# Attention opening in another order, and second-projection weights in dead tiles of keys and queries

## The chip, the core and the metric

The kernel runs on one core of a Trainium2 chip. The metric is the device time of one launch in microseconds (us). The core has five engines with a queue of instructions each: TensorE (PE: matrix products and transposes into PSUM), VectorE (DVE), ScalarE (ACT), GpSimd (POOL) and SyncE (SP), which here only issues DMAs. An engine works its queue in order; an instruction whose inputs are not there holds all that stands behind it. DMAs of one queue are carried out by 16 shared DMA engines.

## The reference

Two layers work on 512 latent tokens and 256 context tokens of 1024 channels. In each layer a modulated RMS norm feeds one projection whose columns go to three groups: Fourier mixing (256 channels), neighbourhood attention (6 heads of 64) and gated linear attention (GLA, 4 heads). The three outputs are joined, go through one output projection with a gated residual, and a modulated norm with a SwiGLU FFN (hidden size 2816) follows. Condensed:

```python
def na_latent(q, k, v, kc, vc, rpb):          # window of the grid + all context keys
    s_loc = einsum('bhrqd,bhrakd->bhrqak', qg, kb) * scale + bias     # masked outside the window
    s_ctx = einsum('bhrqd,bnhd->bhrqn', qg, kc) * scale
    p = jax.nn.softmax(jnp.concatenate([s_loc, s_ctx], -1), axis=-1)
    ...
def fourier_mix(u, w):                        # Re(2-D DFT over positions and group channels)
    return jnp.fft.fftn(z, axes=(1, 3), norm="ortho").real.reshape(B, L, FN_W) @ w
...
x = x + gate * (concat([fourier, attention, gla]) @ w_out)
x = x + gate2 * swiglu(ada_modulate(x))       # the FFN
```

In layer 0 both streams are updated; in layer 1, the last, only the latent one is needed.

## The kernel before

Everything is in fp32. Each product is made of three passes over operands that are split into a high part (ScalarE copies it out as `fp32r`) and a low part (VectorE or GpSimd subtracts the high part): `mm3` (line 183) issues the three, `split` (197) makes the parts. A weight tile is loaded as `raw` (`wraw`, 428) and split into `whl` (`wsplit`, 433), so a weight costs a DMA, an ACT copy and a DVE or POOL subtraction before TensorE can use it.

The output projection is cut in two. The first part, with weights `woa` (five blocks of 128 rows: GLA and Fourier channels), is the generator `wo`; its products are spread over the attention by `fill`, which takes them as filler between the attention's own products. The second part, weights `wob` (three blocks: the attention's channels), is the generator `wb` and runs when the attention is over. Both come from `wout` (969). It makes 8 output tiles `m` for each stream `n`; a product ends with an addition to the residual (`stt`, names `u<-m,u,u` and the like). `raws` are the loaded tiles, two at a time; `part` splits one. In layer 1 `wb` is `whole`: all eight tiles are split beforehand into `whlw`, through two `raw` buffers. In layer 0 it isn't: a tile is split as the one before it is used.

The opening of the attention: line 1111 onward. `next(wo)` issues the first two `woa` loads and the first split; `load_heads` brings keys and queries (`kn`, `qn`, six tiles of 128x512 each) from memory; `load_bias` the position bias; `fourier` (`fn`) makes the Fourier group's features (`ab`, then `pe`, `raw` and `u`), and `stacks_of_heads` (`first`) transposes keys and queries of the first pair of heads and stacks them (`st`). `load_heads("v", vn)` and `load_streams` follow, which load the residual streams `xc` (`u<-in_cxt`) and `xl` (`u<-in_xt`, in layer 1 `u<-xs`). The attention itself goes through 3 pairs of heads in 5 (layer 1: 4) blocks: scores (`a<-st,st`), bias and maximum (`s`, `mx`), exponential (`p`), reciprocal (`rcl`), transposes (`b<-u,p`), copies to `pT`, values (`y<-pT,vn`). While one pair runs, the next pair's keys and queries are prepared (`kt`, `qt`). `kn` and `qn` are dead when the third pair's are prepared.

After the attention the FFN begins: `norm_add` sums squares (`nsq`, `nacc`; for the latent stream of layer 0 on GpSimd), `norm_sums` and `norm_spread` make the norm's factor (`nms`, `nrs`, `ndg`), `nt` and `u<-nt` are the normalised inputs, and `W_first` loads and splits the FFN's first four weight tiles on GpSimd.

The order of the work: on TensorE it is written by hand in the attention and the second projection (`manual_schedule`); on the other engines a scheduler with a model of the times sets it when the program is built. `issue_after` holds instructions back until another one. Pools lay tiles over one another, and a tile that is laid where another was waits until that one is read for the last time.

## Time and profile before

| what | value |
|---|---|
| median of 3 runs | 1663.78 us (1663.53 to 1668.41) |
| profiled execution | 1662.66 us, span 1660.6 us |
| TensorE busy | 1613.8 us (97%) |
| VectorE, ScalarE, GpSimd busy | 920.6 (55%), 583.9 (35%), 232.2 (14%) |
| DMA | 199.66 MB, mean 120 GB/s |
| mean granted TensorE clock | 0.995 |

TensorE is busy nearly all the time, so the time is its work and its pauses. In the slices of the page its share is full in all but the first; the pauses show only in finer windows and in the timeline, where a row's bracket gives the idle time ahead of it and what ended it.

### The profile page before, as it was taken

The page shows a single profiled execution, that of the slowest core. Times are in us where ns is not written, and L with a number is a line of the kernel's source. Part 1 is how long each engine was busy: PE and PEld are TensorE (multiplying, and loading weights), DVE is VectorE, ACT ScalarE, POOL GpSimd, SP SyncE. Part 2 cuts the span into 40 slices and gives each one's busy share as a digit, 9 for nine tenths or more (in the row PEclk, how much of TensorE's full clock was granted, in tenths as well). Part 3 has the DMA queues.
Part 4 walks back from the last instruction along what each step waited for, and adds up shares of the span by engine and source line. Part 5 has one row for each costly group of instructions (what it writes and reads, how often), then busy time and mean ns, then how long its engine had stood idle before and what let it go on. Part 6 is the DMA issues. An engine that isn't in the chain of part 4 may idle for free.

```text
span 1660.6 us, 25071 instructions
## 1 busy us (share of the span) xinstructions
PE 1613.8 (97%) x9938; PEld 1402.3 (84%) x9938; DVE 920.6 (55%) x1665; ACT 583.9 (35%) x1048; POOL 232.2 (14%) x275
## 2 busy tenths in 40 slices
PE   6999999999999999999999999999999999999999
PEld 5878889787888888888888889899787988888887
DVE  5699974776774664355333434464577743434432
ACT  5365223544542411211122324842445522222220
POOL 0143431003240400000000011333102000000000
PEclk9999999999999999999999999999999999999999
DMA  9445544653152454144221411222663233233321
GB/s 329 159 151 164 164 155 124 192 134 112 52 175 76 153 188 143 62 148 146 65 75 45 127 53 40 70 97 94 194 182 119 84 113 99 91 93 98 102 89 51
DMA packets 79904, 199.66 MB, mean 120 GB/s; under 512 B 10344, under 2 KB 21164, under 8 KB 78764
## 3 DMA queue, kind: packets, MB, share of 16 engines
q1 hardware_dynamic: 79788, 198.07, 37.9%
q8 instruction: 78, 1.28, 0.3%
q14 instruction: 38, 0.31, 0.1%
HBM read 174.84 MB, written 14.29 MB: 114 GB/s over the span
## 4 chain that ended last, share of the span: by engine, by line
PE 81%; DVE 7%; DMA 6%; ACT 2%; issue 2%; SPq 1%; POOL 0%; DVEq 0%; ACTq 0%; POOLq 0%
PE a L181 26%; PE m L181 23%; PE b L181 19%; PE y L181 11%; DVE adac L192 2%; DMA adaw<-in_adaw 2%; DVE u L192 1%; DVE whl L189 1%; PE b L1244 1%; DMA raw<-in_wg 1%; DMA raw<-in_wob 1%; DMA raw<-in_w 1%; ACT whl L195 1%; DMA qn<-scr_q 1%; DVE u L189 1%
## 5 line engine op out<-in xcount | busy, mean ns | idle before, releaser
L195 ACT ACTIVATE whl<-raw 128x1024 fp32r<-128x1024 f32 (+7 forms) x222 | 205.0, 928 | 392.2 <-PE a L181 132.3
L189 DVE TENSOR_TENSOR whl<-raw,whl 128x1024 fp32r<-128x1024 f32 (+7 forms) x201 | 225.2, 1122 | 91.7 <-ACT whl L195 91.5
L181 PE MATMUL m<-u,whl 128*128 128x512 f32 (+1 forms) x1278 | 264.1, 359 | 1.9 <-DVE whl L189 1.9
L181 PE MATMUL a<-u,whl 128*128 128x512 f32 (+1 forms) x1299 | 246.6, 346 | 2.4 <-ACT u L195 1.5
L181 PEld LDWEIGHTS m<-u,whl 128*128 128x128 f32 x1278 | 211.9, 191 | 35.3 <-DVE whl L189 2.2
L181 PEld LDWEIGHTS a<-u,whl 128*128 128x128 f32 x1299 | 208.6, 189 | 32.6 <-ACT u L195 1.7
L181 PE MATMUL b<-u,whl 128*128 128x512 f32 (+1 forms) x915 | 181.8, 349 | 1.8 <-ACT whl L195 0.9
L192 DVE SCALAR_TENSOR_TENSOR adac<-adaw,u,adac 128x512 f32<-128x512 f32 x196 | 159.0, 828 | 42.1 <-DMA adaw<-in_adaw 41.0
L181 PEld LDWEIGHTS b<-u,whl 128*128 128x128 f32 x915 | 150.1, 189 | 25.2 <-ACT whl L195 1.1
L181 PE MATMUL b<-whl,u 128*128 128x384 f32 (+1 forms) x696 | 144.9, 345 | 1.3 <-DVE u L192 0.9
L181 PE MATMUL m<-whl,u 128*128 128x384 f32 (+2 forms) x672 | 138.0, 344 | 2.8 <-ACT u L195 2.5
L181 PEld LDWEIGHTS b<-whl,u 128*128 128x128 f32 x696 | 122.2, 189 | 8.7 <-issue 4.7
L181 PEld LDWEIGHTS m<-whl,u 128*128 128x128 f32 x672 | 116.5, 189 | 15.3 <-issue 9.8
L181 PE MATMUL a<-g,whl 128*128 128x512 f32 (+1 forms) x594 | 126.9, 370 | 0.7 <-DVE g L189 0.7
L181 PEld LDWEIGHTS a<-g,whl 128*128 128x128 f32 x594 | 103.9, 189 | 19.8 <-DVE g L189 1.2
L181 PE MATMUL y<-u,whl 128*128 128x512 f32 (+1 forms) x420 | 83.6, 353 | 1.0 <-DVE u L189 1.0
L192 DVE SCALAR_TENSOR_TENSOR ft<-ft,a 128x512 f32<-128x512 f32 (+1 forms) x53 | 30.5, 576 | 95.0 <-ACT ft L195 63.0
L181 PEld LDWEIGHTS y<-u,whl 128*128 128x128 f32 x420 | 69.2, 192 | 12.7 <-DVE u L189 1.4
L181 PE MATMUL m<-g,whl 128*128 128x512 f32 (+1 forms) x396 | 77.8, 350 | 0.0
L181 PEld LDWEIGHTS m<-g,whl 128*128 128x128 f32 x396 | 64.8, 189 | 9.7
L181 PE MATMUL b<-g,whl 128*128 128x256 f32 (+1 forms) x396 | 72.4, 336 | 0.0
L189 POOL TENSOR_TENSOR nacc<-nacc,nsq 128x512 f32<-128x512 f32 (+1 forms) x14 | 15.0, 1074 | 400.2 <-ACT nsq L195 400.2
(220 smaller groups left out, 1983.6 us busy)
## 6 DMA issues: line engine op xcount, KB each, us to landing
raw<-in_w SPq DMA_DIRECT2D x104, 512.0 KB, 3.9
adaw<-in_adaw SPq DMA_DIRECT2D x48, 512.0 KB, 3.8
adaw<-in_adaw SPq DMA_DIRECT2D x64, 256.0 KB, 3.0
raw<-in_wg SPq DMA_DIRECT2D x40, 384.0 KB, 3.4
raw<-in_w SPq DMA_DIRECT2D x32, 448.0 KB, 3.4
adaw<-in_ada SPq DMA_DIRECT2D x8, 1024.0 KB, 10.5
st<-kt SPq DMA_DIRECT2D x32, 192.0 KB, 4.1
raw<-in_woa SPq DMA_DIRECT2D x16, 320.0 KB, 8.8
```

The lines of the kernel that those rows point to most:

```text
L181: last_mm[0] = T.matmul(o, lhsT=l, rhs=r, start=start, stop=stop, skip_group_check=True).ins
L189: e.tensor_tensor(out=o, in0=a, in1=b, op=op)
L192: V.scalar_tensor_tensor(out=o, in0=a, scalar=s, in1=b, op0=op0, op1=op1)
L195: S.activation(out=o, in_=i, func=f, **kw)
L1244: T.transpose(ps[:, 128 * j:128 * j + 128], p[:, 128 * j:128 * j + 128], ident)
```

## The change

The change has five parts. (1) `next(wo)` goes from before the loads of keys and queries to behind those of the bias. (2) With `hold`, the addition of the first product waits for the second product. (3) In layer 1 the queries' transposes are no longer held back behind the Fourier group's last steps. (4) The tags `s`, `p` and `pT` are allocated first in their pool, so `pT` lies elsewhere. (5) `places`: the loads and splits of `wob` use the dead tiles of `kn` and `qn`; in layer 0 five of the eight are split during the attention, tiles 5 and 6 in the buffers of `wo`, and from tile 5 on (before: 6) the products go stream by stream; in layer 1 all eight are loaded without waiting for a buffer.

```diff
+        def place(n):
+            return mk(nap, [128, 512], F32, [f"kn{j}" for j in range(6)][n] if n < 6 else f"qn{n - 6}")
-        def wout(src, nk, streams, kinds, whole=False, split_at=KD, begin=0):
+        def wout(src, nk, streams, kinds, whole=False, split_at=KD, begin=0, places=None, hold=False):
...
+            def raw(m):
+                if places is None:
+                    return wraw(wop, src[m], 128 * nk, 2, cap)
+                r = place(m if whole else m % 2)[:, :128 * nk]
+                nc.sync.dma_start(out=r, in_=src[m])
+                return r
+            def part(r):
+                m = len(w)
+                if places is None or whole or m in (5, 6):
+                    return wsplit(wop, r, (nk, 128), nb, cap, tag)
+                hh, ll = [place(2 + 2 * (m % 5 if m < 5 else 0) + i)[:, :128 * nk].bitcast(F32R) for i in range(2)]
+                split(r, hh, ll)
...
             if whole:
-                w = [part(raw(m)) for m in range(KD)]
+                with tc.issue_after(last_stack[0]):
+                    raws = [raw(m) for m in range(KD)]
+                for r in raws:
+                    w.append(part(r))
+            elif places:
+                raws = [raw(m) for m in range(2)]
+                for m in range(5):
+                    w.append(part(raws[m]))
+                    raws.append(raw(m + 2))
...
-                stt(xs(m), ps, gm(s, m), xs(m), ALU.mult, ALU.add)
+                held.append(lambda: stt(xs(m), ps, gm(s, m), xs(m), ALU.mult, ALU.add))
+                if hold and (m, n) == (0, 0):
+                    return
+                for add in held:
+                    add()
+                held.clear()
...
-        next(wo)
         load_heads("k", kn)
         load_heads("q", qn)
...
             load_bias(nap, h)
+        next(wo)
...
+        for tag, shape, bufs in (("s", [128, 512], 2), ("p", [128, 512], 4), ("pT", [128, 4, 128], 3)):
+            mk(np_, shape, F32, tag, bufs)
...
-        wb = wout(d["wob"][l], 3, streams, "mbmya", not ctx_q, 6 if ctx_q else 0, 0 if ctx_q else 4)
+        wb = wout(d["wob"][l], 3, streams, "mbmya", not ctx_q, 5 if ctx_q else 0, 0 if ctx_q else 4, True)
...
-                if loaded and not ahead:
+                if n == 2 * nb and not ahead:
                     ahead.append(next(wb))
```

Three places show what this moves. The first is SyncE's queue in the opening of layer 0, from the last row of the Fourier tables to the values (`raw<-in_woa` are the first projection's weights). Before:

```order
L1085 DMA pe_3260<-in_nyq 1x258
L430 DMA raw_3108<-in_woa 128x640
L430 DMA raw_3110<-in_woa 128x640
L893 DMA kn_625_3087<-scr_k_35_118 128x1x512
L893 DMA kn_626_3088<-scr_k_35_118 128x1x512
```

and the same stretch after, up to where the two loads now stand:

```order
L1115 DMA pe_3260<-in_nyq 1x258
L893 DMA kn_625_3087<-scr_k_35_118 128x1x512
...
L891 DMA qn_636_3098<-scr_q_37_120 128x512
L1151 DMA bias_3161<-in_rpb 128x512
L1151 DMA bias_3164<-in_rpb 128x512
L430 DMA raw_3167<-in_woa 128x640
L430 DMA raw_3169<-in_woa 128x640
L893 DMA vn_619_3081<-scr_v_36_119 128x1x384
```

The two loads have moved behind all loads of keys, queries and bias. Their splits on ScalarE have moved too, in the same opening; after the change they stand among the feature copies (`u<-m` context features, `ab` latent features, `st` key stacks):

```order
L195 ACTIVATE u_3058<-m_3217 128x256
L195 ACTIVATE whl_3171<-raw_3167 128x640
L195 ACTIVATE u_3059<-m_3218 128x256
L195 ACTIVATE ab_669_3277<-y_3264 128x512
L195 ACTIVATE ab_671_3293<-a_3280 128x512
L195 ACTIVATE whl_3478<-raw_3169 128x640
L195 ACTIVATE st_616_3078<-a_3311 128x256
```

Before, both splits stood eleven and eight rows ahead of `u_3058<-m_3217`, so nothing between these rows waited for a weight.

The second place is GpSimd at the handover from layer 0's second projection to the FFN. `whl` are the first FFN weights' low parts, `nacc` the sums of squares, `nrs` the reciprocal roots. Before:

```order
L189 TENSOR_TENSOR whl_4955<-raw_4953,whl_4955 128x1024
L189 TENSOR_TENSOR whl_4960<-raw_4958,whl_4960 128x1024
L189 TENSOR_TENSOR whl_4965<-raw_4963,whl_4965 128x1024
L189 TENSOR_TENSOR whl_4970<-raw_4968,whl_4970 128x1024
L189 TENSOR_TENSOR nacc_4649<-nacc_4649,nsq_4712 128x512
L189 TENSOR_TENSOR nacc_4649<-nacc_4649,nsq_4745 128x512
```

and after:

```order
L189 TENSOR_TENSOR nacc_4679<-nacc_4679,nsq_4905 128x512
L189 TENSOR_TENSOR nacc_4679<-nacc_4679,nsq_4926 128x512
L189 TENSOR_TENSOR whl_4964<-raw_4962,whl_4964 128x1024
L189 TENSOR_TENSOR whl_4969<-raw_4967,whl_4969 128x1024
L189 TENSOR_TENSOR nrs_5076<-nms_5074,u_63 128x4
L189 TENSOR_TENSOR whl_4974<-raw_4972,whl_4974 128x1024
L189 TENSOR_TENSOR whl_4979<-raw_4977,whl_4979 128x1024
```

The four splits have gone from ahead of the first of seven additions to behind the last.

The third is ScalarE in the third pair of layer 1 (`whlw` are splits of the second projection's weights, `p` exponentials, `pT` copies of transposed probabilities). Before:

```order
L195 ACTIVATE p_12261,sml_12262<-s_12257,nm_12259 128x512
L195 ACTIVATE whlw_12475<-raw_12473 128x384
L195 ACTIVATE pT_12331<-b_12326 128x512
L195 ACTIVATE p_12309,sml_12310<-s_12305,nm_12307 128x512
L195 ACTIVATE whlw_12480<-raw_12478 128x384
L195 ACTIVATE p_12320,sml_12321<-s_12316,nm_12318 128x512
```

and after:

```order
L195 ACTIVATE p_12273,sml_12274<-s_12269,nm_12271 128x512
L195 ACTIVATE whlw_12368<-kn_2207_12352 128x384
L195 ACTIVATE whlw_12371<-kn_2208_12354 128x384
L195 ACTIVATE whlw_12374<-kn_2209_12356 128x384
L195 ACTIVATE whlw_12377<-kn_2210_12358 128x384
L195 ACTIVATE whlw_12380<-kn_2211_12360 128x384
L195 ACTIVATE pT_12343<-b_12338 128x512
L195 ACTIVATE p_12321,sml_12322<-s_12317,nm_12319 128x512
L195 ACTIVATE whlw_12383<-kn_2212_12362 128x384
```

Five splits stand where one stood in front of the copy to `pT`. On VectorE the first product's addition, in the opening of layer 0, has not moved: `u<-m,u,u` 128x256 stands behind `kt<-b` and ahead of the first `rcl` in both.

## Rows read from the trace of the kernel before

**Rows 1.** The page, part 1: the span, and the tensor engine's busy time and instructions.
```profile
span 1660.6 us, 25071 instructions
PE 1613.8 (97%) x9938; PEld 1402.3 (84%) x9938; DVE 920.6 (55%) x1665; ACT 583.9 (35%) x1048; POOL 232.2 (14%) x275
```

**Rows 2.** Windows: stretch, length, PE busy (instructions), granted clock, DMA share, GB/s.
```profile
280.00:300.00 20.00, 19.61 (x148) 1.00 0.75 215
400.00:410.00 10.00, 8.14 (x39) 0.84 0.62 199
1240.00:1250.00 10.00, 8.44 (x69) 1.00 0.82 195
```

**Rows 3.** Timeline, TensorE, layer 0's handover: start, length, what, [idle before, releaser].
```profile
397.51 1.33 PE L181 MATMUL y<-u,whl 128*128 128x256 f32 x9 [0.95 <-DVE u L189]
...
406.02 1.46 PE L181 MATMUL m<-u,whl 128*128 128x256 f32 x8 [1.86 <-DVE whl L189]
...
411.79 2.23 PE L181 MATMUL m<-u,whl 128*128 128x512 f32 x9
...
414.93 2.23 PE L181 MATMUL m<-u,whl 128*128 128x512 f32 x9
...
426.31 2.33 PE L181 MATMUL y<-u,whl 128*128 128x512 f32 x9
...
442.38 3.16 PE L181 MATMUL b<-u,whl 128*128 128x256 f32 x25
445.38 0.86 PE L181 MATMUL m<-u,whl 128*128 128x512 f32 x3
```

**Rows 4.** Timeline, TensorE, layer 1's opening and third pair.
```profile
1200.63 1.19 PE L181 MATMUL a<-st,st 128*128 128x512 f32 x4 [2.83 <-DVE st L192]
...
1249.30 1.20 PE L181 MATMUL a<-st,st 128*128 128x512 f32 x4 [1.56 <-DMA raw<-in_wob]
...
1254.07 1.09 PE L181 MATMUL y<-pT,vn 128*64 128x128 f32 x16
```

**Rows 5.** Timeline, TensorE, layer 0's opening.
```profile
293.38 0.51 PE L181 MATMUL m<-whl,ab 128*128 128x258 f32 x2
...
309.13 0.66 PE L1244 MATMUL b<-u,p 128*128 128x128 f32 x4 [2.90 <-DVE p L1223]
```

**Rows 6.** Timeline, VectorE, layer 0's opening.
```profile
307.52 0.48 DVE L192 SCALAR_TENSOR_TENSOR u<-m,u,u 128x256 f32<-128x256 f32 x1 [0.88 <-DMA u<-in_cxt]
```

**Rows 7.** The chain of waits in the same opening: start, length, what.
```profile
280.68 11.56 DMA qn<-scr_q
...
300.00 7.50 DMA u<-in_cxt
```

**Rows 8.** Timeline, SyncE's DMA issues, same opening.
```profile
271.98 0.25 SPq L1085 DMA_DIRECT2D pe<-in_nyq  x1
275.33 1.01 SPq L430 DMA_DIRECT2D raw<-in_woa  x2
```

**Rows 9.** Timeline, ScalarE, same opening.
```profile
292.71 0.62 ACT L195 ACTIVATE ab<-y 128x512 fp32r<-128x512 f32 x1
```

**Rows 10.** Timeline, VectorE, layer 0's handover.
```profile
403.55 2.42 DVE L189 TENSOR_TENSOR whl<-raw,whl 128x384 fp32r<-128x384 f32 x1 [1.04 <-ACT whl L195]
...
417.99 0.55 DVE L189 TENSOR_TENSOR whl<-raw,whl 128x384 fp32r<-128x384 f32 x1
...
430.58 1.66 DVE L192 SCALAR_TENSOR_TENSOR u<-nt,u,u 128x256 fp32r<-128x256 f32 x2 [0.38 <-ACT u L195]
```

**Rows 11.** Timeline, GpSimd, layer 0's handover.
```profile
403.18 7.69 POOL L189 TENSOR_TENSOR whl<-raw,whl 128x1024 fp32r<-128x1024 f32 x3 [2.74 <-DMA raw<-in_w]
...
430.29 1.27 POOL L189 TENSOR_TENSOR nacc<-nacc,nsq 128x512 f32<-128x512 f32 x1 [1.27 <-ACT nsq L195]
```

**Rows 12.** Timeline, ScalarE, layer 1's third pair.
```profile
1250.04 0.53 ACT L195 ACTIVATE whlw<-raw 128x384 fp32r<-128x384 f32 x1 [3.80 <-DMA raw<-in_wob]
1251.03 0.60 ACT L195 ACTIVATE pT<-b 128x512 f32<-128x512 f32 x1 [0.47 <-PE b L1244]
```

More of the change, by code (lines that the diff above doesn't have):

```diff
@@ L965, in hybrid_kernel @@
         gm = lambda s, k: modT[l][:, s, 16 + k:17 + k]
-        loaded = []
-        def wout(src, nk, streams, kinds, whole=False, split_at=KD, begin=0):
+        def place(n):
+            return mk(nap, [128, 512], F32, [f"kn{j}" for j in range(6)][n] if n < 6 else f"qn{n - 6}")
+        def wout(src, nk, streams, kinds, whole=False, split_at=KD, begin=0, places=None, hold=False):
             nb, cap = (KD, 128 * nk) if whole else (2, 640)
             tag = "whl" + "w" * whole
-            raw = lambda m: wraw(wop, src[m], 128 * nk, 2, cap)
-            part = lambda r: wsplit(wop, r, (nk, 128), nb, cap, tag)
-            if whole:
-                w = [part(raw(m)) for m in range(KD)]
+            def raw(m):
[10 more added lines that the diff above has]
+                split(r, hh, ll)
+                return [a.rearrange("p (a b) -> p a b", a=nk) for a in (hh, ll)]
+            w = []
+            if whole:
+                with tc.issue_after(last_stack[0]):
[7 more added lines that the diff above has]
+                    raws.append(raw(m + 2))
             else:
                 raws = [raw(m) for m in range(2)]
-                w = [part(raws[0])]
+                w.append(part(raws[0]))
             early = {}
@@ L1003, in product @@
                         yield None, ps.shape[-1]
-                stt(xs(m), ps, gm(s, m), xs(m), ALU.mult, ALU.add)
+                held.append(lambda: stt(xs(m), ps, gm(s, m), xs(m), ALU.mult, ALU.add))
[4 more added lines that the diff above has]
+                held.clear()
+            held = []
             todo = [(m, n) for m in range(split_at) for n in range(len(streams))]
@@ L1010, in wout @@
             for m, n in todo:
-                if m == KD - 1:
-                    loaded.append(src)
-                if m + 1 == len(w) < KD:
-                    w.append(part(raws[m + 1]))
-                    if m + 2 < KD:
-                        raws.append(raw(m + 2))
+                if len(w) <= m + (2 if places else 1) and len(w) < KD:
+                    w.append(part(raws[len(w)]))
+                    if len(raws) < KD:
+                        raws.append(raw(len(raws)))
                 yield from product(m, n, *streams[n])
@@ L1021, in hybrid_kernel @@
         both_x = lambda yc, yl: ([(yc, lambda m: xc[m], 1)] if ctx_q else []) + [(yl, lambda m: xl[m], 0)]
-        wo = wout(d["woa"][l], 5, both_x(ya(ygc, yfc) if ctx_q else None, ya(ygl, yfl)), "m")
+        wo = wout(d["woa"][l], 5, both_x(ya(ygc, yfc) if ctx_q else None, ya(ygl, yfl)), "m", hold=ctx_q)
         fst = ExitStack()
@@ L1132, in hybrid_kernel @@
             next(first)
-        for _ in range(2):
-            next(fn)
-        with tc.issue_after(last_mm[0]):
+        if ctx_q:
+            for _ in range(2):
+                next(fn)
+            with tc.issue_after(last_mm[0]):
+                for _ in first:
+                    pass
+        else:
             for _ in first:
```

## The prediction

> **What bounds the kernel now.** I read the page's first two parts, then the table of 10 us windows, and only then the rows of the windows that stand out. TensorE is busy for 1613.8 of 1660.6 us [rows 1], so all its pauses together come to 46.8 us, and a change to the attention stages can only win back the pauses that lie there. The windows show where: the opening of layer 0's attention (300 to 320 us), the handover from layer 0's second projection to its FFN (400 to 440), and the same two places of layer 1 (1190 to 1210, 1240 to 1290). In the first three stands a pause of about 2 us or more, and with it a window whose mean granted clock is about 0.84 of full [rows 2], so that part of it runs at 1.2 instead of 2.4 GHz. A mean of 0.84 over 10 us is 1.6 us of lost work. So the pause of 1.86 us [rows 3], like the longer ones, costs its length and 1.6 us; the one of 1.56 us at 1249.30 [rows 4] stands in a window at 1.00. The level is one of the clock, and the pause ahead of it is all that the rows show of its cause.
>
> In the opening the pause is 2.90 us before the transposes of the probabilities [rows 5]; VectorE has them late, and its own last wait there is 0.88 us for a context tile from memory [rows 6], which the chain follows back over DMAs to the loads of queries [rows 7]. In the handover the largest is 1.86 us before a product of the second projection [rows 3], released by a VectorE split.
>
> My terms are sums against the profiled execution, 1662.66 us with a span of 1660.6. The median of the three runs shown is 1663.78, 1.1 us above it, and I add that at the end.
>
> **Layer 0, opening.** Before, the sync queue issued a small table row at 271.98, waited for TensorE, issued the two loads of first-projection weights at 275.33 [rows 8], and the loads of the keys behind them. Now keys, queries and bias go first. They can start right behind the table row, at 272.3; the two weight loads come behind all of them. TensorE is busy for 19.6 of the 20 us from 280 to 300 [rows 2], so earlier keys gain nothing there by themselves: its products of Fourier features fill the time in any order. What may be gained is the 0.88 us wait, since the values and the context tiles move forward in the same queue. What is lost: the weight splits now stand on ScalarE ahead of the second feature copy (`u<-m`) and of `ab<-y` and `ab<-a`. Keys, queries and bias are 3.7 MB, fourteen tiles of 128x512 in all; at the 215 GB/s of 280 to 300 [rows 2], with the two table loads before them still on their way, they are through at about 291, and the first weight tile (320 KB, 1.5 us) with about 1.5 us until its landing is known is there at 293 to 295. ScalarE's place for the split is about a microsecond ahead of `ab<-y`, begun at 292.71 [rows 9]. It waits 2 to 3 us, and then the split itself delays `ab<-y` as well. TensorE takes that copy into `m<-whl,ab`, whose first products stood at 293.38 [rows 5]. I take a loss of 2.9 us there and a gain of 0.9 from the context wait: **+2.0 us**. Bounds: -0.9 (the weights land in time) and +5.5 (they are 2 us later still and the clock falls).
>
> The held addition is costed at nothing. In VectorE's order the first product's `u<-m,u,u` stands where it stood, behind the key copy and ahead of the reciprocal; holding it moves it past nothing. The 2.90 us pause therefore stays, up to the 0.9.
>
> **Layer 0, attention.** Five of the eight splits of second-projection weights move from the handover into pairs 1 and 2: 0.55 us each on VectorE without company [rows 10], and about as much on ScalarE. The windows show no pause of TensorE in those pairs, so slack covers them; where it doesn't, at most 5 x 0.55 = 2.8. I take **+0.3**.
>
> **Layer 0, handover.** The eight pairs of products of the second projection repeat every 3.14 us, by the starts at 411.79 and 414.93 [rows 3]; 8 x 3.14 = 25.1 from 397.5, and 0.4 for a column sum between them, end at 423.0. Before, they ended at 426.31 + 2.33 = 428.6 [rows 3]. So 5.6 us of pauses and slow clock go. What is late next: VectorE, ScalarE and GpSimd then finish the sum of squares (the last addition ended at 431.6, 2.9 us after the last product [rows 3, 11]), and only then does GpSimd begin the four splits of the FFN's first weights; before they stood ahead of all seven additions, now behind. Each takes 7.69 / 3 = 2.56 us [rows 11]. Start at 425.9: ready at 428.5, 431.0, then, with a small reciprocal root of about 1.2 us between, 434.8 and 437.4. TensorE needs 3.1 us for the 24 or 25 products of each [rows 3]: the last ends at about 440.5, and with the norm's small products and the clock after a 5 us pause the wide products of the FFN (`m<-u,whl` 128x512) start at 442.2, against 445.38 [rows 3]. **-3.2 us.** The earlier FFN loads (their tiles no longer wait for the last transposed probabilities) gain nothing, as their splits are late. Bounds: -6 (GpSimd's splits start sooner) and 0.
>
> Here a row speaks against the change. A VectorE split of 128x384 took 2.42 us while GpSimd was splitting, 0.55 without; two normalising additions took 1.66 together while GpSimd added [rows 10]. The Trainium skill, page "GPSIMD Engine Reference", section "Specifications", says that GpSimd's path to the on-chip memory is shared with VectorE, with contention where a VectorE instruction has two inputs there. The trace agrees, 2.42 against 0.55. By that rule the four late splits would run beside VectorE's sixteen normalising operations, where before they ran beside the projection.
>
> **Layer 1, opening.** The pause of 2.83 us [rows 4] is released by VectorE's scaled copy of the queries, which waits behind the first Fourier result's split and its wait for ScalarE. With the queries' transposes ahead, it stands behind one weight split instead: about **-0.8**; bounds -1.5 (the dip is milder) and +0.5 (weights late, as in layer 0).
>
> **Layer 1, attention.** Before, each of the eight loads waited for an earlier split; and the first split of ScalarE waited 3.80 us for its own [rows 12]. Now all eight are issued at once, and ScalarE's order has five splits in a row in front of the copy `pT<-b`. The first lands as before, at 1250.0. At the 195 GB/s of that window [rows 2] each 192 KB takes 1.0 us, so ScalarE ends the fifth at 1254.6 and `pT` comes 3.6 us after its 1251.03 [rows 12]. TensorE took it at 1254.07, 2.4 us after it was ready [rows 4], so 1.2 us show; the exponentials behind it are late by about as much again. Against this ScalarE's seven later waits for these loads fall away. I take **+0.8**, bounds -1.5 and +4. The 1.56 us pause at 1249.30 [rows 4] lies ahead of these loads and stays. The Trainium skill, page "DMA: Bandwidth & Descriptors", section "Anatomy of one DMA", has the variable part of a DMA at bytes / 436 GB/s, an estimate of 0.45 us apiece here; by it the five would follow at ScalarE's own pace and the term would be -0.8. The trace's 195 GB/s speaks against it.
>
> Sum: +2.0 + 0.3 - 3.2 - 0.8 + 0.8 = -0.9; 1662.66 - 0.9 = 1661.8 on the profiled basis, **1662.9 us** on that of the median.
>
> **Rivals.**
> A, the opening is cured. If earlier keys and values let VectorE reach the probabilities 2 us sooner, the pause falls under 1 us and the dip goes with it: 2.0 + 1.6 = 3.6 gained in place of the 2.0 lost: 1662.9 - 2.0 - 3.6 = 1657.3. For it: the chain runs from the query loads to the context load [rows 7]. Against: VectorE's order is unchanged there, and TensorE's products between fix the time at which it may start.
> B, slower: the weights land late in layer 0. If their load takes the 11.56 us of the query load from an issue at about 285 [rows 7], it is there at 296.5, ScalarE stands for 5 us, and the dip of 1.6 follows: opening +2.9 + 2.2 + 1.6 - 0.9 = +5.8, in all 1666.7. It decides from a loss of 2.9 us in the opening, where the total passes the median of before. For it: one order of ScalarE holds three copies behind the split. Against: nothing but the bias lies between queries and weights.
> C, contention in the handover. Eight normalising additions at 0.83 instead of 0.43 us [rows 10] add 3.2 us, and the gain there is 0: 1666.1. For it: the two halves of rows 10. Against: TensorE waits for the splits anyway, which covers most.
> D, layer 1's five splits cost their upper bound and a dip: 1662.9 + 3.2 = 1666.1, within what can be measured.
>
> **Chances.** The forecast 0.50, with its own range 1659 to 1667; A 0.18, with what else goes well in the handover; B 0.15; C 0.10; D 0.07. This kernel's measurement tells 0.3%, 5.0 us, from no change. Under 1658.8 lie A with its neighbours and the forecast's lower end: 0.27. Over 1668.8 lie parts of B, C and D, alone or together: 0.17. The rest, 0.56, is within. The range 1655.5 to 1669.5 reaches A's side by more than B's, since the handover's bound of -6 adds to it.
>
> **What would show it.** Right: a wait of ScalarE for `raw<-in_woa` near 292 with TensorE pausing for `ab`; the pause before `b<-u,p` still over 1.5 us; no pause within the second projection of layer 0, then one of about 5 us until GpSimd's first split, and `m<-u,whl` 128x512 starting 2 to 4 us sooner relative to the projection's start; five `whlw` splits of ScalarE in a row, with waits for memory. Wrong: no wait for those weights (A), GpSimd's splits well over 2.6 us beside VectorE (C), or the wide products of the FFN starting more than 47 us after the projection's first (445.38 - 397.51 = 47.9 before [rows 3]).

## The result, and the profile after

The changed kernel takes 1676.08 us (median of 7 runs, 1675.31 to 1683.45), the kernel before 1663.78 (7 runs, 1662.35 to 1668.55). The ratio is 1.0080, with a 95% interval of 1.0065 to 1.0095: it is 12 us slower, where no change was forecast (1662.9, range 1655.5 to 1669.5). Its profiled execution took 1675.63 us.

The page of the changed kernel, part 1, and the line of part 3 that will matter below:

```profile
span 1673.8 us, 25074 instructions
PE 1616.2 (97%) x9938; PEld 1404.6 (84%) x9938; DVE 922.9 (55%) x1665; ACT 584.0 (35%) x1048; POOL 232.3 (14%) x275
...
q8 instruction: 78, 1.28, 0.3%
```

The span is 13.2 us longer than in [rows 1], with the same products on TensorE and the busy times of the other engines within 2.3 us. So it is waiting, and TensorE's slower clock behind the waits: the span less TensorE's busy time, which is its pauses, went from 46.8 to 57.6 us, and the same products took 2.4 us longer. Starts of the same TensorE instructions in both timelines show where it came in; the last column is the gain or loss since the line above.

| TensorE instruction | before | after | later by | added |
|---|---|---|---|---|
| layer 0, first transposes of probabilities (`b<-u,p`) | 309.13 | 312.28 | 3.15 | +3.15 |
| layer 0, second projection begins | 397.51 | 402.81 | 5.30 | +2.15 |
| layer 0, first 128x512 product of the FFN | 445.38 | 453.16 | 7.78 | +2.48 |
| layer 1, a product of its first projections | 993.60 | 1000.94 | 7.34 | -0.44 |
| layer 1, first head sum of the linear attention | 1122.82 | 1133.07 | 10.25 | +2.91 |
| layer 1, first scores | 1200.63 | 1210.68 | 10.05 | -0.20 |
| layer 1, third pair | 1249.30 | 1259.49 | 10.19 | +0.14 |
| layer 1, first product of the second projection | 1272.16 | 1285.38 | 13.22 | +3.03 |

Five places lost 2.1 to 3.2 us each, and none gained as much as half a microsecond. One of the five, the linear attention of layer 1, is not touched by the change.

**Layer 0, opening.** TensorE after (start, length, what, [idle before, releaser]), against [rows 5], and below it ScalarE after:

```profile
295.81 0.82 PE L181 MATMUL m<-whl,ab 128*128 128x258 f32 x2 [3.51 <-ACT ab L195]
...
312.28 0.66 PE L1280 MATMUL b<-u,p 128*128 128x128 f32 x4 [1.94 <-DVE p L1259]
```

```profile
294.26 0.74 ACT L195 ACTIVATE whl<-raw 128x640 fp32r<-128x640 f32 x1 [3.10 <-DMA raw<-in_woa]
```

ScalarE stands 3.10 us for the weights, and TensorE 3.51 us for the copy behind them. The old pause of 2.90 is still there, at 1.94. Windows after (stretch, length, TensorE busy with its instructions, mean granted clock, DMA share, GB/s), here and for one later place:

```profile
290.00:300.00 10.00, 6.23 (x39) 0.85 0.75 232
...
310.00:320.00 10.00, 7.56 (x42) 0.83 0.01 3
...
430.00:440.00 10.00, 6.17 (x30) 0.68 0.25 77
```

The same two windows of the opening before:

```profile
290.00:300.00 10.00, 9.85 (x77) 1.00 0.78 216
...
310.00:320.00 10.00, 9.71 (x61) 0.83 0.35 79
```

Only one of them was below 1.00; now both are, so part of each ran at 1.2 GHz instead of 2.4.

**Layer 0, pairs and handover.** In the pairs ScalarE waits for a weight whose load had to wait for one of the two load tiles:

```profile
359.38 0.53 ACT L195 ACTIVATE qn<-kn 128x384 fp32r<-128x384 f32 x1 [4.26 <-DMA kn<-in_wob]
```

TensorE after, against [rows 3]:

```profile
368.56 1.31 PE L181 MATMUL a<-st,st 128*128 128x512 f32 x4 [1.17 <-DMA st<-qt]
...
402.81 1.33 PE L181 MATMUL y<-u,kn 128*128 128x256 f32 x9 [0.95 <-DVE u L189]
...
426.80 2.31 PE L181 MATMUL y<-u,kn 128*128 128x512 f32 x9
433.02 0.38 PE L181 MATMUL a<-u,whl 128*128 128x256 f32 x1 [3.91 <-ACT whl L195]
...
435.47 4.00 PE L181 MATMUL a<-u,whl 128*128 128x256 f32 x17 [0.81 <-POOL whl L189]
...
441.77 3.26 PE L181 MATMUL a<-u,whl 128*128 128x256 f32 x25 [1.14 <-DVE u L192]
...
453.16 0.73 PE L181 MATMUL m<-u,whl 128*128 128x512 f32 x2 [1.60 <-ACT u L195]
```

What the pairs lost, they lost at the turn to the third pair: up to the scores at 354.74 the products stand 3.14 us later than before, from those at 374.87 on 5.30 us. The projection now runs without a pause: from 402.81 to the end of its last group, 429.1, it takes 26.3 us, where before it took 31.1 [rows 3]. Then come 3.91 us of waiting for the FFN's first weights, further pauses of 0.81, 1.14 and 1.60 us, and a slow stretch, at 0.68 from 430 to 440 [window above], where before the projection's pause stood in a window at 0.84 [rows 2]. ScalarE begins the first of their splits only here:

```profile
431.93 1.04 ACT L195 ACTIVATE whl<-raw 128x1024 fp32r<-128x1024 f32 x1
```

GpSimd's low halves follow at 433.05, and VectorE's normalising operations meet them:

```profile
433.05 4.88 POOL L189 TENSOR_TENSOR whl<-raw,whl 128x1024 fp32r<-128x1024 f32 x2 [1.01 <-ACT whl L195]
437.89 1.21 POOL L189 TENSOR_TENSOR nrs<-nms,u 128x4 f32<-128x4 f32 x1
439.07 4.92 POOL L189 TENSOR_TENSOR whl<-raw,whl 128x1024 fp32r<-128x1024 f32 x2
```

```profile
433.68 2.02 DVE L192 SCALAR_TENSOR_TENSOR u<-nt,u,u 128x256 fp32r<-128x256 f32 x1 [0.18 <-ACT u L195]
...
436.20 2.01 DVE L192 SCALAR_TENSOR_TENSOR u<-nt,u,u 128x256 fp32r<-128x256 f32 x1
...
438.64 0.48 DVE L192 SCALAR_TENSOR_TENSOR u<-nt,u,u 128x256 fp32r<-128x256 f32 x1
...
439.30 2.42 DVE L192 SCALAR_TENSOR_TENSOR u<-nt,u,u 128x256 fp32r<-128x256 f32 x1 [0.18 <-ACT u L195]
```

The same operation takes 0.48 us between GpSimd's splits and 2.0 to 2.4 beside one. The three long ones end at 435.70, 438.21 and 441.72; GpSimd's splits end at 435.5, 437.9 and 441.5 (halves of the rows of two). Each ends 0.2 to 0.3 us behind a split, as if it had waited for the split's end. The Trainium skill, page "SBUF — State Buffer", section "SBUF: two separate sides", says that VectorE and GpSimd take their common port in turn and that the one that comes later waits for the whole instruction of the other; these ends agree with that.

**Layer 1, third pair.** ScalarE and, below, VectorE after, against [rows 12]:

```profile
1260.39 2.08 ACT L195 ACTIVATE whlw<-kn 128x384 fp32r<-128x384 f32 x4 [4.11 <-DMA kn<-in_wob]
1262.64 0.53 ACT L195 ACTIVATE whlw<-kn 128x384 fp32r<-128x384 f32 x1 [0.17 <-DMA kn<-in_wob]
1263.07 0.58 ACT L195 ACTIVATE pT<-b 128x512 f32<-128x512 f32 x1
```

```profile
1260.95 1.08 DVE L189 TENSOR_TENSOR whlw<-kn,whlw 128x384 fp32r<-128x384 f32 x2 [3.95 <-ACT whlw L195]
1261.95 0.68 DVE L1248 CUSTOM_DVE_ANT_0 s<-a,bias 128x512 f32<-128x512 f32 x1
...
1263.64 1.02 DVE L189 TENSOR_TENSOR whlw<-kn,whlw 128x384 fp32r<-128x384 f32 x2
...
1270.18 0.48 DVE L1259 TENSOR_SCALAR p<-p,rcl 128x512 f32<-128x512 f32 x1
```

Four splits of ScalarE follow each other without a gap and the fifth waits 0.17 us, so the weights came on average at most 0.56 us apart and memory did not space them. VectorE has the low half of each split. It idles 3.95 us for the first, but that is not new; VectorE before:

```profile
1250.59 0.56 DVE L189 TENSOR_TENSOR whlw<-raw,whlw 128x384 fp32r<-128x384 f32 x1 [3.64 <-ACT whlw L195]
...
1255.14 0.49 DVE L1223 TENSOR_SCALAR p<-p,rcl 128x512 f32<-128x512 f32 x1
```

New is how many halves stand close together. From 1260.95 on VectorE does eight of them, about 0.55 us each, ahead of the second scaling of the probabilities (`p<-p,rcl`), where before it did two. This scaling comes 10.7 us after the pair's first scores instead of 5.8, and TensorE waits for it:

```profile
1268.19 0.63 PE L1280 MATMUL b<-u,p 128*128 128x128 f32 x4 [0.67 <-DVE rcl L1258]
...
1270.80 0.63 PE L1280 MATMUL b<-u,p 128*128 128x128 f32 x4 [1.98 <-DVE p L1259]
```

**Layer 1, linear attention.** ScalarE's order there is that of before. It waits longer for one load of gate weights, and TensorE for what follows from it. Before, and then after, ScalarE and TensorE:

```profile
1077.18 0.84 ACT L195 ACTIVATE whl<-raw 128x768 fp32r<-128x768 f32 x1 [2.61 <-DMA raw<-in_wg]
...
1083.78 0.92 PE L181 MATMUL a<-u,u 128*128 128x192 f32 x4 [1.16 <-DVE u L192]
```

```profile
1086.16 0.85 ACT L195 ACTIVATE whl<-raw 128x768 fp32r<-128x768 f32 x1 [4.28 <-DMA raw<-in_wg]
...
1092.52 1.65 PE L181 MATMUL a<-u,u 128*128 128x192 f32 x4 [2.25 <-DVE u L192]
```

TensorE's pause is 1.1 us longer, and behind it the mean granted clock is 0.83 from 1092 to 1102 us, where it was 1.00 before (1083 to 1093): another 1.7 us.

### The profile page after: what moved, and what is told of

Same layout as the page of the kernel before. It is cut to its first block, busy times and chain, and to the rows that moved or that the text cites. A ratio compares the mean times of both kernels' runs of the same rounds, so it can differ in the third digit from the quotient of the medians.

```text
span 1673.8 us, 25074 instructions
## 1 busy us (share of the span) xinstructions
PE 1616.2 (97%) x9938; PEld 1404.6 (84%) x9938; DVE 922.9 (55%) x1665; ACT 584.0 (35%) x1048; POOL 232.3 (14%) x275
## 5 line engine op out<-in xcount | busy, mean ns | idle before, releaser
L195 ACT ACTIVATE whl<-raw 128x1024 fp32r<-128x1024 f32 (+6 forms) x214 | 201.1, 943 | 386.5 <-PE a L181 129.9
L189 DVE TENSOR_TENSOR whl<-raw,whl 128x1024 fp32r<-128x1024 f32 (+6 forms) x193 | 218.7, 1134 | 94.7 <-ACT whl L195 93.8
L181 PE MATMUL m<-u,whl 128*128 128x512 f32 (+1 forms) x1233 | 256.0, 360 | 1.6 <-ACT u L195 1.6
L181 PE MATMUL a<-u,whl 128*128 128x512 f32 (+1 forms) x1281 | 242.8, 347 | 5.9 <-ACT whl L195 3.9
L181 PEld LDWEIGHTS m<-u,whl 128*128 128x128 f32 x1233 | 205.1, 191 | 34.2 <-ACT u L195 1.8
L181 PE MATMUL b<-u,whl 128*128 128x512 f32 (+1 forms) x897 | 177.5, 350 | 0.7 <-DVE u L192 0.7
L181 PE MATMUL m<-g,whl 128*128 128x512 f32 (+1 forms) x396 | 77.8, 350 | 0.0
L181 PE MATMUL y<-u,whl 128*128 128x512 f32 (+1 forms) x393 | 76.7, 348 | 0.0
L181 PEld LDWEIGHTS y<-u,whl 128*128 128x128 f32 x393 | 63.7, 189 | 10.4 <-issue 0.8
```

The source lines that it names most:

```text
L181: last_mm[0] = T.matmul(o, lhsT=l, rhs=r, start=start, stop=stop, skip_group_check=True).ins
L189: e.tensor_tensor(out=o, in0=a, in1=b, op=op)
L195: S.activation(out=o, in_=i, func=f, **kw)
```

## The experiments

The stretches named here are those of the table: opening (up to `b<-u,p`, from a head sum at 268.09 before and 267.72 after: 41.04 and 44.56 us), pairs (to the second projection: 88.38 and 90.53), handover (to the FFN: 47.87 and 50.35), linear attention of layer 1 (129.22 and 132.13), third pair of layer 1 (22.86 and 25.89). Ratios are against the kernel before on the same chip.

**e1, the weights of the first projection loaded early again**

```
+        next(wo)
         load_heads("k", kn)
...
             load_bias(nap, h)
-        next(wo)
```

> The changed kernel with the first projection's two weight loads and first split put back ahead of the loads of keys and queries; all else as changed. Theory (the weights arrive behind 3.7 MB and ScalarE waits for them in front of two feature copies): the 3.51 us pause before the products with `ab` and the clock dip with it go, the 0.9 us at the probabilities comes back, so the opening is 3 us shorter and the time about 1673 us; the later losses stay. Rival (the opening is bound by VectorE's chain to the probabilities, so the pause only moves there): 1675 to 1676 us.

Measured: 1672.85 us, ratio 1.0048 (1.0032 to 1.0064); the opening is back at 41.42 us, without the pause for `ab`. The move of these loads costs what the opening lost.

**e2, the kernel before with that move alone**

```
-        next(wo)
         load_heads("k", kn)
...
             load_bias(nap, h)
+        next(wo)
```

> The kernel before with that one move alone (weight loads behind keys, queries and bias). Theory: ScalarE waits about 3 us for the weights at 291 to 294, TensorE pauses 3.5 us, and the time is 3 us over that of before, about 1667 us; nothing after the opening changes. Rival (earlier keys pay for it once the rest of the change is away): 1663 us or less.

Measured: 1670.28 us, ratio 1.0028 (1.0013 to 1.0044). In its profile ScalarE and TensorE stood longer than in that of the changed kernel (ScalarE, then TensorE):

```profile
297.81 0.74 ACT L195 ACTIVATE whl<-raw 128x640 fp32r<-128x640 f32 x1 [5.78 <-DMA raw<-in_woa]
```

```profile
299.36 1.02 PE L181 MATMUL m<-whl,ab 128*128 128x258 f32 x2 [6.19 <-ACT ab L195]
...
316.01 0.66 PE L1244 MATMUL b<-u,p 128*128 128x128 f32 x4 [1.94 <-DVE p L1223]
```

The opening took 47.43 us, everything else within 0.8 us of what it took before. When the weights are there varies: from the last table row's issue to the split it took 22.4 us in the changed kernel and 25.1 here, and most of the difference lies ahead of the weights' own issue on SyncE (15.6 and 18.0 us behind the table row). With the late loads the opening was 44.6 to 47.5 us in eight profiles; in the six kernels that load them early it was 40.3 to 42.1.

**e3, layer 0's second projection as before**

```
-        wb = wout(..., 5 if ctx_q else 0, 0 if ctx_q else 4, True)
+        wb = wout(..., 6 if ctx_q else 0, 0 if ctx_q else 4, None if ctx_q else True)
```

The moment at which layer 0's generator is started is that of before too.

> The changed kernel, but in layer 0 the second projection's weights are loaded and split as before, through two buffers, and its products are cut at tile 6 again; layer 1 as changed. Theory: the 2.1 us lost in layer 0's attention (ScalarE waits 4.26 us for a weight load in the third pair's preparation) and the 2.0 to 2.5 us lost at the handover (GpSimd's four splits late and beside VectorE's normalising additions) go: about 1671.5 us. Rival (the handover's own pauses of before, 5.6 us, come back and cost as much as they did): 1673 to 1676 us, the attention alone gaining 2.

Measured: 1671.09 us, ratio 1.0030 (1.0017 to 1.0043). Pairs 88.37, handover 47.95, and the linear attention of layer 1 is back at 129.08. So without the dead tiles of layer 0 the pairs and the linear attention lose nothing. The handover is a weaker case: in the FFN behind it two pauses of 1.35 and 0.87 us came at 770 us, which no edit touches, and from the second projection's start to layer 1's first projections e3 took 599.5 us, the changed kernel 598.1 and the kernel before 596.1. The held product and the score tiles taken in advance are still in this kernel, and its pairs show no cost of them; they were not run alone, and neither was part (3).

**e4, layer 1's second projection as before**

```
-        wb = wout(..., 5 if ctx_q else 0, 0 if ctx_q else 4, True)
+        wb = wout(..., 5 if ctx_q else 0, 0 if ctx_q else 4, True if ctx_q else None)
```

> The changed kernel, but in layer 1 the eight tiles of the second projection go through two buffers as before, in turn; layer 0 as changed. Theory: the pauses of 0.52, 0.67 and 1.98 us in layer 1's third pair go and the three short ones of before come back: 2.5 to 3 us less, about 1673 us. Rival (the third pair is late because its queries are, whose DMA ends the 1.70 us pause there): no difference, 1676 us.

Measured: 1677.94 us, ratio 1.0067 (1.0043 to 1.0092), which does not set it apart from the changed kernel; in its profile the opening took 47.5 us. The third pair does set it apart: it takes 23.60 us instead of 25.89, and the pauses for `rcl` and `p` are gone. TensorE:

```profile
1262.21 1.20 PE L181 MATMUL a<-st,st 128*128 128x512 f32 x4 [1.55 <-DMA raw<-in_wob]
1273.34 1.45 PE L181 MATMUL y<-pT,vn 128*64 128x128 f32 x16 [1.04 <-DVE u L189]
...
1285.81 1.67 PE L181 MATMUL m<-u,whlw 128*128 128x256 f32 x12
```

**e5, the FFN's first splits on VectorE**

```
-            W_first = [w13(u, (G, G)) for u in range(2)]
+            W_first = [w13(u) for u in range(2)]
```

> The changed kernel with the four low-half splits of the FFN's first weights in both layers on VectorE instead of GpSimd. Theory (GpSimd's splits slow VectorE's normalising operations in layer 0's handover): u<-nt,u,u 128x256 goes from 2.02 back to about 0.48 us, each split takes about 1.2 us on VectorE instead of 2.44 on GpSimd, and from the second projection's start to the first 128x512 product of the FFN it takes 47.5 to 48.5 us instead of 50.35; total about 1673.5. Rival (the wait is for ScalarE, which begins its own first split only at 431.9, and GpSimd's company costs nothing): that stretch stays within 0.5 us of 50.35, or is longer by VectorE's own four splits (5 us), total 1676 to 1679.

Measured: 1683.32 us, ratio 1.0108 (1.0085 to 1.0130). In layer 0 it went as the theory said: handover 48.50 us, a split 1.2 us, and the normalising operations beside them 0.48. VectorE:

```profile
435.29 1.21 DVE L189 TENSOR_TENSOR whl<-raw,whl 128x1024 fp32r<-128x1024 f32 x1
436.43 0.48 DVE L192 SCALAR_TENSOR_TENSOR u<-nt,u,u 128x256 fp32r<-128x256 f32 x1
```

TensorE's pause of 3.91 us before the first FFN product stays, as the rival had it: it is ScalarE's. The pauses of 0.81 and 1.14 us behind it, for GpSimd's half and for VectorE's slowed operation, are gone. Of the 1.85 us gained, how much is contention and how much the faster split is not shown, and some of TensorE's products stand in another order. Up to layer 1's first projections the gain is lost again, to pauses of 0.91 and 0.87 us at 773 us: 598.2 us from the second projection's start, 598.1 in the changed kernel. The total is worse because layer 1 has the same splits on VectorE too: from its second projection to the FFN's normalisation it takes 26.3 us instead of 18.1.

**e8, the same edit in the kernel before**

> The kernel before with the four low-half splits of the FFN's first weights in both layers on VectorE instead of GpSimd. Theory (the contention costs the kernel before too, inside its second projection, where a VectorE split of 2.42 us instead of 0.55 goes ahead of a pause of 1.86 us and a slow clock): the handover of 47.87 us becomes 46 to 47, total 1662 to 1663. Rival (there GpSimd's splits lie beside work that hides them, and VectorE's 5 us more come on top): 48.5 to 50, total 1665 to 1667.

Measured: 1671.05 us, ratio 1.0039 (1.0025 to 1.0052). Layer 0's handover fell to 45.17 us, more than expected; layer 1 gave it back and more. TensorE there:

```profile
1292.19 1.01 PE L181 MATMUL a<-u,nacc 128*128 128x1 f32 x4 [6.50 <-DVE nacc L189]
```

VectorE's splits stand ahead of the projection's additions and the last sum of squares.

**e9, four weights of layer 0 and four load tiles**

```
-                r = place(m if whole else m % 2)[:, :128 * nk]
+                r = place(m)[:, :128 * nk]
...
-                hh, ll = [place(2 + 2 * (m % 5 if m < 5 else 0) + i)...
+                hh, ll = [place(4 + 2 * (m % 6) + i)...
```

Weights 0 to 3 are loaded into places of their own, later ones as in layer 0 before.

> The changed kernel with four instead of five weights of layer 0's second projection in dead tiles, and four load tiles instead of two, so that the four loads follow each other and none waits for an earlier split. Theory (in layer 0's pairs ScalarE stands 4.26 us at a split whose load waited for one of the two load tiles, and the probabilities and query copies behind it are late): that wait goes, and the stretch from b<-u,p to the second projection goes from 90.5 back to 88.4 to 89.0 us; total about 1674.3. Rival (it is the splits' own time among the pairs): 4 of 5 of the 2.15 us stay, 90.1 us, total 1675.7.

Measured: 1674.86 us, ratio 1.0065 (1.0042 to 1.0089). ScalarE's wait of 4.26 us is gone, and the pairs still take 90.38 us. My theory fell. TensorE now pauses 1.09 us for VectorE's query copy, which two splits precede:

```profile
359.96 0.63 PE L1281 MATMUL b<-u,p 128*128 128x128 f32 x4 [1.09 <-DVE qt L192]
...
370.82 1.19 PE L181 MATMUL a<-st,st 128*128 128x512 f32 x4 [0.68 <-DMA st<-qt]
```

**e14, the same with the splits behind all query copies**

```
-                raws = [raw(m) for m in range(4)]
+                with tc.issue_after(last_stack[0]):
+                    raws = [raw(m) for m in range(4)]
```

> The changed kernel with four of layer 0's second-projection weights in dead tiles, whose loads are issued only behind the last query stack's, so that their splits stand behind all query copies of pair 3 on ScalarE and VectorE. Theory (in the pairs it is the place of these splits, in front of the query copies of pair 3, that costs 2 us, not their own time and not the load tiles): from b<-u,p to the second projection 88.3 to 88.8 us instead of 90.4. Rival (the four splits' time on VectorE and ScalarE costs wherever it stands): 89.8 to 90.5.

Measured in one run: 1673.83 us, pairs 89.84. The rival's figure again. The pause has moved to the next thing that VectorE has late:

```profile
373.54 1.09 PE L181 MATMUL y<-pT,vn 128*64 128x256 f32 x8 [1.24 <-DVE u L189]
```

So the splits cost among the pairs at either of the two places tried (the loads without the splits were not run): in all eight profiles with them the pairs took 89.6 to 90.5 us, in all six without 88.1 to 88.4.

**e10, what the runs until then pointed to**: first-projection weights early, e9's tiles, e5's splits, layer 1 as before.

> What the runs so far point to together: the first projection's weights loaded as before (ahead of keys and queries), layer 0's dead tiles with four load tiles, the FFN's first splits on VectorE, and layer 1's second projection as before. Theory: opening 41.4, body 88.6, handover 46 to 48 against 47.87 before, layer 1's third pair as before; if the 2.9 us in layer 1's linear attention come with the dead tiles of layer 0 as in all three runs that had them, total 1663 to 1667, without them 1661 to 1664. Rival (dead tiles cost in themselves, wherever the splits stand): body 90 and handover 50, total 1669 or more.

Measured: 1681.05 us, ratio 1.0089 (1.0066 to 1.0112). Opening 40.33, but pairs 90.29 and handover 48.78: the rival. Layer 1 lost 6.8 us to VectorE's splits as in e8, and 5.3 in its opening to query loads (four pauses of 0.62 to 1.58 us for `qn<-scr_q`); why these came late in this profile stays open.

**e11, the kernel before with layer 0's splits on VectorE**

```
-            W_first = [w13(u, (G, G)) for u in range(2)]
+            W_first = [w13(u, (V, V) if ctx_q else (G, G)) for u in range(2)]
```

> The kernel before with the four low-half splits of the FFN's first weights on VectorE in layer 0 alone (layer 1 keeps them on GpSimd). Theory (the contention in layer 0's handover costs the kernel before too, and what the run with both layers lost was layer 1's, where VectorE's splits put 6.5 us of waiting for the norm's sum in front of TensorE): handover 45.2 us as in that run, against 47.87, everything else as before; span 1658, total 1661 to 1662, 0.1 to 0.2% below before. Rival (the 2.7 us is given back later): total 1664 and more.

Measured: 1662.61 us, ratio 0.9993 (0.9982 to 1.0004). Layer 1 is as before (18.2 us), which confirms where e8 lost; the handover is 47.40 us and not e8's 45.17. The largest pause of the projection fell from 1.86 us [rows 3] to 0.71, but of the gain almost nothing shows: behind a pause of 1.52 us the granted clock was 0.66 from 429 to 439 us, 3.4 us of lost work, where e8, with the same pause, has 1.00 in this window. Why the clock fell in one and not in the other is not shown. It is no faster than can be measured, and none of the kernels beat the one before.

**e12, the kernel before with three small products at its very beginning**

```
+    more = [3]
+
     def mm3(o, lh, ll, rh, rl, start, stop):
+        while start and more[0]:
+            more[0] -= 1
+            mm(o[..., :128], lh, rh[..., :128], True, False)
```

> The kernel before with three small products (128 columns) more at its very beginning, whose result is overwritten; nothing else is moved. It shifts every later block of 16,384 bytes that TensorE's sequence of instructions is fetched in. Theory (in layer 1's linear attention such a fetch of 0.95 us stands on one of 16 DMA engines ahead of the last part of a weight load, and how many instructions TensorE has ahead of that place decides whether it does: 9 wait instructions fewer or more do not matter, but the kernels with 4 to 6 more are all hit): the stretch from the landmark product at 993.6 to the GLA's first head sum goes from 129.2 to 132 us. Rival (it hangs on the dead tiles of layer 0 in another way): 129.2 as before.

Measured in one run: 1665.70 us, span 1663.6, 3.0 us more than before, though single runs of the kernel before lie between 1659.7 and 1669.2 us in the same series. The linear attention of layer 1 takes 131.96 us instead of 129.22, as in the changed kernel. ScalarE:

```profile
1078.82 0.85 ACT L200 ACTIVATE whl<-raw 128x768 fp32r<-128x768 f32 x1 [4.25 <-DMA raw<-in_wg]
```

Nothing near this place had changed. The packets of the three traces, in us after the table's product of layer 1 (993.60, 1000.94, 993.63):

| | instruction packet, 16,384 bytes | the load's 15th and 16th end marks (4 bytes) | ScalarE starts |
|---|---|---|---|
| before | 83.03 to 83.99 | 83.04, 83.14 | 83.58 |
| after | 83.13 to 84.07 | 83.09, 84.08 | 85.22 |
| e12 | 83.10 to 84.08 | 83.14, 84.41 | 85.19 |

The load closes with sixteen packets of 4 bytes. The Trainium skill, page "DMA: Bandwidth & Descriptors", section "Why a DMA increments its semaphore by 16 and not by 1", says that each DMA engine writes such a mark behind its own share of the data and that only the last one ends the wait; the table agrees. Before, all sixteen are through when the instruction packet has just begun; in the other two, the sixteenth ends behind it, and ScalarE starts behind that. The packet's 0.95 us explain the first part of ScalarE's 1.6 us; the rest, ScalarE's 0.8 to 1.1 us after the last mark where it had been 0.44, is not explained.

The other profiles fit: in all eight with the longer stretch the sixteenth mark ends behind the packet (by 0.0 to 1.3 us), in the other six it ends within 0.3 us of the packet's start. But a packet begins at 82.8 to 83.3 us in thirteen of the fourteen (81.4 in e9), hit or not, and the three products did not move it (83.03 and 83.10). So its time does not decide; on which of the sixteen DMA engines it stands is not in the record.

**e13, the changed kernel with six such products**

> The changed kernel with six small products (128 columns) more at its very beginning, whose result is overwritten. Theory (fetch and weight load meet by their place in TensorE's sequence): the collision is left behind, and the same stretch of layer 1 goes from 132.1 back to 129.2 us. Rival (it hangs on the dead tiles): 132 stays.

Measured in one run: 1674.65 us, and the stretch stays at 131.92. A miss: the collision was not left behind. e12 shows that it can come without any of the change; that the number of TensorE's instructions decides was not shown, with one kernel for it, one against it and each profiled once. Free of it are the five other kernels without layer 0's tiles (129.1 to 129.3 us) and e14 (129.9).

This profile shows something else: its handover took 47.19 us, less than before, with the changed kernel's projection, the same pause of 3.91 us and GpSimd's splits in place. Two VectorE operations of 2.0 us stand beside the splits; the third one missed them (0.48 us), and the pause of 1.14 us is absent. The scheduler also put the products with `ndg` ahead of the last 47 narrow products, where the changed kernel has them behind, and the pause of 1.60 us is absent too. TensorE:

```profile
437.18 4.00 PE L181 MATMUL a<-u,whl 128*128 128x256 f32 x17 [0.87 <-POOL whl L194]
...
445.22 1.05 PE L181 MATMUL a<-ndg,u 128*128 128x128 f32 x8
446.02 5.88 PE L181 MATMUL b<-u,whl 128*128 128x256 f32 x47
451.74 0.86 PE L181 MATMUL m<-u,whl 128*128 128x512 f32 x3
```

e4, with TensorE's order of the changed kernel, took 50.36 us there; e1, e9 and e14 48.7 to 49.0. So 2.7 of the changed kernel's 50.35 us are pauses that the same work can do without.

## Why the prediction was wrong

By its own steps, forecast against measured:

- **Layer 0, opening, +2.0 against +3.2.** The mechanism was right in each part: ScalarE had the weights at 294.3 (293 to 295 forecast), it stood 3.10 us for them (2 to 3), and the context wait gave back 0.96 (0.9). The size was off in one term: the new pause brought a slow stretch of its own (0.85), which the forecast allowed only in its upper bound, while the old pause, still 1.94 us, kept its slow stretch (0.83). e1 and e2 show that the move does it. Rival B's +5.8 describes e2's profile, where the weights came at 297.8 and the opening lost 6.4 us.
- **Layer 0, pairs, +0.3 against +2.15.** The step that failed is "the windows show no pause of TensorE in those pairs, so slack covers them". A window without a pause says that the operands came in time, not by how much; VectorE was busy for 64.7 of the 90 us from 310 to 400 before. The bound of 2.8, five splits at 0.55, was near; the loss stayed without the wait for a load tile (e9) and with the splits at another place (e14).
- **Layer 0, handover, -3.2 against +2.5.** The largest miss. The projection lost its pauses as forecast (4.8 us of the 5.6), and the wait behind it came nearly as forecast: TensorE had GpSimd's first half 32.7 us behind the projection's start, where the forecast had 31.0, and a half took 2.44 us (2.56). The step that failed is "the last ends at about 440.5", with the wide products at 442.2: TensorE was to follow the four splits without another wait, 13.7 us from the first split to the wide products, 1.7 of them for the clock and the norm's small products. It took 17.7 us: TensorE paused again for VectorE (1.14) and for ScalarE (1.60), and its mean granted clock was 0.86 over this stretch, which is 2.5 us. The 1.14 us are rival C, the contention; for them the sentence that TensorE "waits for the splits anyway, which covers most" was wrong. The 1.60 us hang on TensorE's order (e13). So the size of the loss, and even its sign, is that of one order of the work, but no kernel with the changed projection came under 47.2 us where the forecast had 44.7. ScalarE's first half stands behind squares and normalising copies; why it comes that late, with its load already issued, was not settled.
- **Layer 1, opening, -0.8 against -0.2.** The pause fell from 2.83 to 2.16 us, and the slow stretch stayed. Over all kernels the term looks right: this stretch took 76.5 to 78.1 us in the eight with the transposes ahead (median 77.1), 77.8 to 78.2 in four without (median 78.0); e8 and e10, with VectorE's splits and late query loads, are left out.
- **Layer 1, third pair, +0.8 against +3.0.** Inside the bounds, but by another path. The step that failed is that each weight takes 1.0 us and ScalarE's copy to `pT` is what comes late: the weights came on average at most 0.56 us apart, and ScalarE's splits ran at their own pace of 0.52. The 195 GB/s of [rows 2] are what that window moved, with loads that waited for each other, and not what memory can give. The Trainium skill's page "DMA: Bandwidth & Descriptors", section "Anatomy of one DMA", which the forecast had weighed and set aside, was nearer with an estimate of 0.45 us apiece, though it writes of DMAs from GpSimd's queue and these come from SyncE's; yet the term did not become -0.8. The forecast followed ScalarE and put VectorE's halves at nothing: eight instead of two of 0.55 us stood ahead of the second scaling, 3.3 us more. e4 and e10, without the tiles, have 23.6 and 23.3 us.
- **Linear attention of layer 1, not in the sum, +2.9.** The rows of before hold nothing that this term could have come from; e12 shows it without any of the change.

The five terms of the sum missed by 1.2, 1.9, 5.7, 0.6 and 2.2 us, all to the slow side. The bounds held four of them; the handover's ended at 0, and no bound stood for layer 1's linear attention.

## What to carry to other kernels

A stretch in which TensorE never pauses has no slack that can be read from TensorE: before work is moved into it, follow the engine that feeds it in program order, and count the moved work nearly in full if that engine is busy most of the time. When a load is moved behind others, price the pause that it makes and the slow clock behind it, and take its landing from the latest of several runs. Follow both halves of a split operation: here ScalarE's queue set the start and VectorE's queue carried the harm. Before a loss of 2 or 3 us in one profile is given a cause, see how the same code fared in the profiles of other kernels.

## What the runs showed of the hardware that was not expected

- A VectorE operation of 0.48 us took 2.0 to 2.4 beside GpSimd's splits of 2.44 us and ended 0.2 to 0.3 us behind them, as if it had waited for the whole instruction. A split that costs GpSimd 2.44 us costs VectorE 1.2.
- In a kernel with three products more at its start, a stretch some 1080 us later took 2.7 us longer (e12), where an instruction packet of 0.95 us met the end of a weight load. Profiles of kernels that differ in nothing near a place can differ there by 3 us, 0.2% of the time.
- The same loads in the same queue order were there 22.4 to 25.1 us behind the last table row's issue, in eight kernels.
- Behind the same pause of 1.52 us the granted clock was 0.66 over ten us in e11 and 1.00 in e8.
